# Column sums and row factors in two token halves, a split weight transfer and selection products at the beginning of a hybrid transformer layer

## The chip, the cores and the metric

The kernel runs on one core of a Trainium2 chip. A core has a matrix engine (TensorE, PE in the rows, with its weight loads shown as PEld), VectorE (DVE), ScalarE (ACT), GpSimd (POOL) and SyncE (SP), which here only issues transfers. Each engine works through its own list of instructions in order, and semaphores between the lists carry the dependencies. The metric is the time of one execution on the device in microseconds; the time of a version is the median of several runs.

## What is computed

One layer of a diffusion backbone over 512 latent tokens (x) with 256 context tokens (ctx), 1024 channels. The part that matters here is its start: both streams are normalised by their root mean square and modulated by two vectors per channel that come from a small product with the conditioning vector.

```python
def _rmsnorm(x, gain):
    xf = x.astype(jnp.float32)
    y = xf * lax.rsqrt(jnp.mean(xf * xf, axis=-1, keepdims=True) + EPS)
    return y.astype(x.dtype) * gain

def _modulate(x, gain, shift, scale):
    return _rmsnorm(x, gain) * (1 + scale) + shift

...
    mod = jax.nn.silu(c) @ w_ada[l] + b_ada[l]
    mod_c = jax.nn.silu(c_ctx) @ w_ada[l] + b_ada[l]
    sh1, sc1, g1, sh2, sc2, g2 = jnp.split(mod[:, None, :], 6, axis=-1)
    csh1, csc1, cg1, csh2, csc2, cg2 = jnp.split(mod_c, 6)
    a_lat = _modulate(x, norm_mix[l], sh1, sc1)
    a_ctx = _modulate(xc, norm_mix[l], csh1, csc1)
...
```

Behind that come a combined input projection, a pooling mixer, a bidirectional chunkwise mLSTM, an output projection and a SwiGLU network. The change touches none of these.

## The kernel before

**Layout.** Everything is kept with channels on the 128 partitions and tokens along the free dimension; the 1024 channels are eight blocks of 128, numbered k. Large products are made with three products of split operands (high and low parts), so each weight block and each activation block is split by ScalarE (the high part, a cast) and VectorE (the low part, a subtraction).

**Loads.** SP issues, in the order of the program: the parameter table parm (L104), x in four transfers of two blocks each (L132), the 128x128 identity ident (L137), and then alternately the modulation weights of a block (tile ada, 1 MB, L267) and the first projection weights of a block (tile wr, 384 KB, L330), as far as their three buffers each allow, and the context blocks (tile cx, L381). Before the data arrive, PE multiplies a zero tile by itself (keep_warm, L143); it has shorter groups of such products between its later steps.

**The manual section.** From L255 on, the order of the instructions on PE, ScalarE and VectorE is the one in which the program writes them, until `manual.__exit__`. Outside it a planner orders them. SP and GpSimd are not part of it.

**The sums of squares.** ScalarE squares blocks 0 to 6 of x (L347). VectorE adds squares 1 to 5 to that of block 0 (L349), squares block 7 itself (L350) and adds square 6 to it (L351). PE sums the two results over the channels, with the squares as weights and two columns of ones as the moving operand (L354): for each of four groups of 128 tokens, a column that holds the sum for each token. `power` scales and shifts these (L235, VectorE) and raises them to -1/2 on GpSimd (L237). `rstd_rows` (L245) turns the four columns into a row of 512 factors on all partitions, by a product of the broadcast column with ident.

**The modulation vectors.** For a block k, `mod_rows` (L271) multiplies the activated conditioning vectors of both streams with the block's weights; the eight products of a block lie in four strips of 32 rows of a bank, with four products for r = 0 and four for r = 1 accumulated on them. ScalarE copies the bank out (L274). In `mod_cols`, two transposes on PE (L280) bring it back to channels on partitions, VectorE adds the four strips (L282), and two further operations add the bias and form shift (shm, L284) and scale (sm, L285).

**A stage.** `stage` issues the load of the block's projection weights and splits them (L331, L333); `modulate` forms the normalised and modulated block (L291 on VectorE, L292 on ScalarE for the high part, L295 on VectorE for the low part). `products` (L339) are the first six tiles of the projection, accumulated over the eight blocks in six banks. The loop over k runs the products of block k, with `mod_rows`, `mod_cols` and `stage` of block k + 2 among them.

Of the kernel before, what the change touches and what calls it, by code (L numbers as in the profile page):

```python
# [10 lines left out]
F32 = mybir.dt.float32  # L11
F32R = mybir.dt.float32r
AF = mybir.ActivationFunctionType
ALU = mybir.AluOpType
# [3 lines left out]
P = 128  # L18
D = 1024
KT = D // P  # L20
T = 512
# [19 lines left out]
C_NM, C_NF, C_NFIN = 0, 8, 16  # L41
C_CW, C_CB = 24, 72
C_PS, C_MG, C_C, C_CC, C_BA = 88, 96, 104, 112, 120
NPAR = 168
U0, Q0, K0, O0, G5, G6 = 0, 8, 16, 24, 32, 40
WARM = (32, 2, 2, 2, 0)
# [4 lines left out]
def layer_kernel(ctx: ExitStack, tc, xT, cT, w0, w1, wv0, wv, wada_a, wada_b, par, crow, bg, wpool,  # L51
                 wout, wffi, wffo, icnt, consts, out):
    nc = tc.nc
    V = nc.vector
# [16 lines left out]
    def tl(tag, shape, dtype=F32, bufs=1, align=None):  # L71
        cnt[0] += 1
        return homes[tag].tile(shape, dtype, name=f"{tag}_{cnt[0]}", tag=tag, bufs=bufs, align_bytes=align)

    def S(tag, dtype=F32):
        return tl(tag, [P, T], dtype, BUFS[tag], HALFLINE if tag in shifted else LINE)
# [4 lines left out]
    def PS(tag="ps"):  # L81
        cnt[0] += 1
        return ps.tile([P, 512], F32, name=f"{tag}{cnt[0]}", tag=tag, bufs=4)
# [7 lines left out]
    def small(shape, nm, dtype=F32, home="small"):  # L91
        return homes[home].tile(shape, dtype, name=nm, tag=nm, bufs=1)
# [8 lines left out]


    parm = small([P, NPAR], "parm")
    nc.sync.dma_start(parm, par)  # L104

    def pcol(base, j):
        return parm[:, base + j:base + j + 1]
# [5 lines left out]
    warm = small([P, P], "warm", home="x")  # L113
# [6 lines left out]
    bsc1 = small([P, KT], "bsc1")  # L120
# [8 lines left out]
    x_sb = []  # L129
# [4 lines left out]
    ones = small([P, P], "ones")  # L134
    nc.gpsimd.memset(ones, 1.0)
    ident = small([P, P], "ident")
# [4 lines left out]
    def keep_warm(n, zero):  # L141
        for i in range(n):
            nc.tensor.matmul(wbank[:, :zero.shape[-1]], zero, zero, start=True, stop=True)  # L143
# [52 lines left out]
    class SumSq:  # L196


        q = None
# [51 lines left out]
    ALL = slice(0, T)  # L251
    HALF = (slice(0, T // 2), slice(T // 2, T))
# [4 lines left out]
    stx = SumSq()  # L257
# [2 lines left out]
    mods = small([P, 48], "mods")  # L260
    sm = small([P, KT, 2], "sm")
    shm = small([P, KT, 2], "shm")

    def mod_rows(k):

        raw = tl("ada", [P, KT, 256], F32, 3)
        nc.sync.dma_start(raw.rearrange("p k c -> p (k c)"), wada_a[k])  # L267
        acc = PS()
        for r in range(2):
            for g in range(4):  # L270
                nc.tensor.matmul(acc[32 * g:32 * g + 32, :256], sil[:, 4 * r + g, :], raw[:, 4 * r + g, :],  # L271
                                 start=r == 0, stop=r == 1, tile_position=(0, 32 * g))
        rows = S("tmp")
        nc.scalar.copy(rows[:, :256], acc[:, :256])  # L274
        return rows

    def mod_cols(k, rows):
        bank = PS()
        for w in range(2):
            nc.tensor.transpose(bank[:, w * P:(w + 1) * P], rows[:, w * P:(w + 1) * P], ident)  # L280
        both = tl("rc2", [P, 2, 2], F32, 2)
        V.tensor_reduce(both, bank[:, :2 * P].rearrange("p (w g j) -> p w j g", w=2, g=4)[:, :, 0:2, :],  # L282
                        mybir.AxisListType.X, ALU.add)
        V.tensor_scalar(shm[:, k, :], both[:, 0, :], pcol(C_BA, k), None, ALU.add)  # L284
        V.tensor_scalar(sm[:, k, :], both[:, 1, :], bsc1[:, k:k + 1], pcol(C_NM, k), ALU.add, ALU.mult)  # L285

    def modulate(src, r, scale, shift, h, l, between=None):

# [37 lines left out]
    def stage(k, r):  # L326

        n = len(FIRST) * P
        raw, wh, wl = tl("wr", [P, WMAX], F32, 3), tl("wh", [P, WMAX], F32R, 2, LINE), tl("wl", [P, WMAX], F32R, 2, LINE)
        nc.sync.dma_start(raw[:, :n], w0[k])  # L330
        nc.scalar.copy(wh[:, :n], raw[:, :n])  # L331
        aT.append(modulate(x_sb[k], r, sm[:, k, 0:1], shm[:, k, 0:1], S("a", F32R), S("a", F32R),
                           lambda: V.tensor_sub(wl[:, :n], raw[:, :n], wh[:, :n].bitcast(F32))))  # L333
        w_first.append([(wh[:, i * P:(i + 1) * P], wl[:, i * P:(i + 1) * P]) for i in range(len(FIRST))])
# [9 lines left out]
    bank = PS()  # L344
    sq = [S("tmp") for _ in range(KT)]
    for k in range(KT - 1):
        nc.scalar.activation(sq[k], x_sb[k], AF.Square)  # L347
        if 0 < k < KT - 2:
            V.tensor_add(sq[0], sq[0], sq[k])  # L349
    V.tensor_mul(sq[KT - 1], x_sb[KT - 1], x_sb[KT - 1])  # L350
    V.tensor_add(sq[KT - 1], sq[KT - 2], sq[KT - 1])  # L351
    for t, q in enumerate((sq[0], sq[KT - 1])):
        for i in range(T // P):
            nc.tensor.matmul(bank[:, 2 * i:2 * i + 2], q[:, i * P:(i + 1) * P], ones[:, 0:2], start=t + i == 0,  # L354
                             stop=t == 1, skip_group_check=True)
        if t == 0:
            keep_warm(WARM[1], warm)
    sd = stx.power(bank, T // P)
    rows = mod_rows(0)
    keep_warm(WARM[2], warm)  # L360
    mod_cols(0, rows)
    r = stx.rstd_rows(sd, ALL)
    stage(0, r)
    keep_warm(WARM[3], warm)
    rows = mod_rows(1)
    keep_warm(WARM[4], warm)
    products(0, 0, nf, ((0, 0),))
    mod_cols(1, rows)
    nc.scalar.copy(rs_x, r)
    stage(1, rs_x)  # L370
    for k in range(KT):
        parts = ((0, 0), (0, 1), (1, 0))[0 if k else 1:]
        products(k, 0, nf // 2, parts)
        if k + 2 < KT:
            rows = mod_rows(k + 2)
        products(k, nf // 2, nf, parts)
        if k + 2 < KT:
            mod_cols(k + 2, rows)
            stage(k + 2, rs_x)
        if k < 4:  # L380
            nc.sync.dma_start(cxt[k], cT[:, k * 512:(k + 1) * 512])  # L381
            for e in range(2):
                stc.add(c_sb[2 * k + e], slice(0, TC))
        if k == 4:
            sd = stc.rstd_cols(slice(0, TC))
        if k == 5:
            nc.scalar.copy(rs_c[:, :TC], stc.rstd_rows(sd, slice(0, TC)))
        if k == KT - 2:
            wv_first = vload(wv0, DH + NG, 0)
        if k in (5, 6):  # L390
            ctx_quad(4 * (k - 5))
# [612 lines left out]
    def prepare(j):  # L1004

        a = tl("wr", [P, WMAX], F32, 3)[:, :D]
        b = tl("ur", [P, D], F32, 2)
        nc.sync.dma_start(b, wffi[2 * j + 1])
        nc.sync.dma_start(a, wffi[2 * j])
        a11, a12, a21, a22 = a[:, :T], a[:, T:], b[:, :T], b[:, T:]  # L1010
        p = {}

        def direct(nm, w, dram=None):
            h, l = S("oh", F32R), S("ol", F32R)
            nc.scalar.copy(h, w)
            if dram is None:
                V.tensor_sub(l, w, h.bitcast(F32))
            else:
                nc.scalar.activation(l, w, AF.Copy, scale=-1.0)  # L1019
                nc.gpsimd.dma_start(l, dram, accum_op=ALU.add)  # L1020
            p[nm] = ptiles(h, l)

        def summed(names, o, h, l):
            split(sg[:, o:o + D], h, l)
            for e, nm in enumerate(names):
                p[nm] = ptiles(h, l, e * T)

        yield
        sg = tl("sg", [P, 2 * D], F32, 1, LINE)
        s1, s2, s3, s4 = (sg[:, i * T:(i + 1) * T] for i in range(4))  # L1030
        direct("A11", a11)
        V.tensor_add(s1, a22, a21)
        V.tensor_add(s2, s1, a11)
        summed(("S1", "S2"), 0, wide("gh"), wide("gl"))
        yield
        direct("A12", a12, wffi[2 * j][:, T:])
        yield
        V.tensor_add(s3, a11, a21)
        V.tensor_add(s4, s2, a12)
        yield  # L1040
        summed(("S3", "S4"), D, *(tl(t, [P, WMAX], F32R, 2, LINE)[:, :D] for t in ("wh", "wl")))
        yield
        direct("A22", a22, wffi[2 * j + 1][:, T:])
        yield p
# [70 lines left out]
    sd = st1.rstd_cols(HALF[0])  # L1115
# [3 lines left out]
    r = st1.rstd_rows(sd, HALF[0])  # L1119
# [37 lines left out]
    with tc.manual_schedule(engines={mybir.EngineType.PE, mybir.EngineType.Activation, mybir.EngineType.DVE}):  # L1157
# [3 lines left out]
        sd = st1.rstd_cols(HALF[1])  # L1161
        e.up()
        r = st1.rstd_rows(sd, HALF[1])
# [35 lines left out]
        p = prepare(NP)  # L1199
# [86 lines left out]
    sd = st2.rstd_cols(HALF[0])  # L1286
# [5 lines left out]
    sd = st2.rstd_cols(HALF[1])  # L1292
# [92 lines left out]
```

## Time and profile before

| | |
|---|---|
| median of 3 runs | 887.99 us (887.89 to 888.52) |
| profiled execution, its own time | 889.47 us |
| span of the profiled execution, first to last instruction | 887.7 us |
| mean granted PE clock | 0.999 |
| instructions | 15037 |
| moved by DMA | 120.87 MB, mean 136 GB/s |
| DMA in the first 40 us | 14.70 MB, mean 367 GB/s |

The span is the time between the first and the last instruction of one execution; the execution's own time has something around that. In the rows, `out<-in` names the tiles that an instruction writes and reads, followed by their shapes, a count and durations in microseconds or nanoseconds as stated; `[0.99 <-PE pat L339]` is the idle time of the engine ahead of the instruction and what ended it. The chain is the work that ended last, followed back from the end: each piece is there because the next one waited for it or stood behind it on the same engine. A line number can be that of a helper that several callers use.

### The profile page before, as it was taken

Reading aid. Unit: us, or ns where it says so; the run is one execution under the profiler, and the core shown is the slowest. Engines: PE = TensorE matmul, PEld = TensorE weight load, DVE = VectorE, ACT = ScalarE, POOL = GpSimd, SP = SyncE. Lnnn points to the kernel's source line nnn. Section 1 sums busy time; section 2 is a strip of 40 time slices with the busy share of each in tenths; the row PEclk is TensorE's granted clock in tenths of the full one; section 3 lists DMA queues with packets and bytes.
Section 4 is the critical chain, followed back from the end, with each engine's and each line's share of the span. In section 5 each row is a group of like instructions: output and inputs, shape, how many; then the busy total and the mean of one; then the engine's idle time right before and its main releaser. Section 6 shows DMA issues by size and latency. Waiting matters only on the chain.

```text
span 887.7 us, 15037 instructions
## 1 busy us (share of the span) xinstructions
PE 875.4 (99%) x5920; PEld 796.9 (90%) x5920; DVE 613.8 (69%) x1187; ACT 434.5 (49%) x823; POOL 66.6 (8%) x93
## 2 busy tenths in 40 slices
PE   8999999999999999999999999999999999999996
PEld 7689798899888998889988899999889998899996
DVE  4678676877876787767876767884376753867644
ACT  4464363545345453354545446773146741666542
POOL 0000010010000100001000000110011100111000
PEclk9999999999999999999999999999999999999999
DMA  9853022436252632525443830484266643765402
GB/s 347 324 196 111 25 72 61 166 111 174 75 196 74 196 114 83 163 98 161 137 132 119 286 118 2 128 204 108 83 178 144 155 108 100 196 144 128 135 1 95
DMA packets 41445, 120.87 MB, mean 136 GB/s; under 512 B 4480, under 2 KB 8864, under 8 KB 40352
## 3 DMA queue, kind: packets, MB, share of 16 engines
q1 hardware_dynamic: 35904, 109.96, 38.5%
q0 software_dynamic: 5472, 9.96, 6.7%
q8 instruction: 46, 0.75, 0.3%
q14 instruction: 23, 0.19, 0.1%
HBM read 116.22 MB, written 3.69 MB: 135 GB/s over the span
## 4 chain that ended last, share of the span: by engine, by line
PE 87%; DVE 6%; ACT 3%; DMA 2%; issue 1%; POOL 0%; DVEq 0%; SPq 0%; ACTq 0%; POOLq 0%
PE ps L187 20%; PE ps L188 19%; PE ps L189 19%; PE pat L339 3%; PE ps L571 3%; PE ps L570 3%; PE ps L572 3%; PE pat L187 2%; PE pat L188 2%; PE pat L786 2%; PE pat L189 2%; PE pat L785 2%; PE pat L784 2%; PE ps L339 1%; PE pat L745 1%
## 5 line engine op out<-in xcount | busy, mean ns | idle before, releaser
L157 ACT CAST wh<-wr 128x1024 fp32r<-128x1024 f32 (+3 forms) x78 | 78.8, 1011 | 114.6 <-PE ps L188 87.3
L187 PE MATMUL ps<-a,wh 128*128 128x512 f32 x320 | 125.3, 391 | 0.0
L188 PE MATMUL ps<-a,wh 128*128 128x512 f32 x320 | 124.9, 390 | 0.0
L189 PE MATMUL ps<-a,wl 128*128 128x512 f32 x320 | 124.8, 390 | 0.0
L158 DVE TENSOR_TENSOR wl<-wr,wh 128x1024 fp32r<-128x1024 f32 (+3 forms) x78 | 91.8, 1176 | 43.3 <-ACT wh L157 41.9
L189 PE MATMUL ps<-act,wl 128*128 128x512 f32 (+1 forms) x224 | 77.7, 347 | 0.9 <-DVE wl L158 0.9
L187 PE MATMUL ps<-act,wh 128*128 128x512 f32 (+1 forms) x224 | 77.7, 347 | 0.1
L188 PE MATMUL ps<-act,wh 128*128 128x512 f32 (+1 forms) x224 | 77.5, 346 | 0.0
L189 PEld LDWEIGHTS ps<-a,wl 128*128 128x128 f32 x320 | 60.1, 188 | 12.6
L187 PEld LDWEIGHTS ps<-a,wh 128*128 128x128 f32 x320 | 60.1, 188 | 12.0
L188 PEld LDWEIGHTS ps<-a,wh 128*128 128x128 f32 x320 | 60.1, 188 | 11.6
L1020 POOL DMA_DIRECT2D ol<-in_wffi x38 | 33.4, 887 | 256.1 <-ACT ol L1019 91.6
L187 PE MATMUL ps<-hp,gh 128*128 128x256 f32 x176 | 50.1, 284 | 1.6 <-ACT pat L1058 1.5
L1229 DVE SCALAR_TENSOR_TENSOR x<-ps,lb,x 128x512 f32<-128x512 f32 (+1 forms) x32 | 19.6, 616 | 44.0 <-PE ps L189 43.9
L187 PE MATMUL ps<-hp,oh 128*128 128x256 f32 x176 | 48.9, 278 | 0.1
L189 PE MATMUL ps<-hp,gl 128*128 128x256 f32 x176 | 48.9, 278 | 0.0
L188 PE MATMUL ps<-hp,gh 128*128 128x256 f32 x176 | 48.9, 278 | 0.0
L188 PE MATMUL ps<-hp,oh 128*128 128x256 f32 x176 | 48.7, 277 | 0.0
L189 PE MATMUL ps<-hp,ol 128*128 128x256 f32 x176 | 48.5, 277 | 0.0
L189 PEld LDWEIGHTS ps<-act,wl 128*128 128x128 f32 x224 | 42.2, 188 | 6.8 <-DVE wl L158 1.6
L187 PEld LDWEIGHTS ps<-act,wh 128*128 128x128 f32 x224 | 42.2, 188 | 5.5 <-issue 0.3
L188 PEld LDWEIGHTS ps<-act,wh 128*128 128x128 f32 x224 | 42.2, 188 | 5.3
(341 smaller groups left out, 2629.8 us busy)
## 6 DMA issues: line engine op xcount, KB each, us to landing
wr<-in_w SPq DMA_DIRECT2D x42, 512.0 KB, 3.6
pb<-in_wada_b SPq DMA_DIRECT2D x32, 512.0 KB, 4.2
wr<-in_wffi SPq DMA_DIRECT2D x25, 512.0 KB, 4.2
ur<-in_wffi SPq DMA_DIRECT2D x19, 512.0 KB, 3.9
ol<-in_wffi POOLq DMA_DIRECT2D x38, 256.0 KB, 4.9
ada<-in_wada_a SPq DMA_DIRECT2D x8, 1024.0 KB, 9.5
wr<-in_wffo SPq DMA_DIRECT2D x16, 448.0 KB, 3.5
wr<-in_wout SPq DMA_DIRECT2D x8, 512.0 KB, 3.6
```

The lines of the kernel that those rows point to most:

```text
L157: nc.scalar.copy(wh, raw[:, :n])
L158: V.tensor_sub(wl, raw[:, :n], wh.bitcast(F32))
L187: nc.tensor.matmul(dst, wh, ah, start=first and i == 0, stop=False, skip_group_check=on)
L188: nc.tensor.matmul(dst, wh, al, start=False, stop=False, skip_group_check=on)
L189: nc.tensor.matmul(dst, wl, ah, start=False, stop=last and i == n - 1, skip_group_check=on)
L339: nc.tensor.matmul(acc0[i], w_first[k][i][w], aT[k][x], start=k + w + x == 0, stop=k == KT - 1 and w == 1)
L570: nc.tensor.matmul(acc[:, :n], ah, wh, start=kk == 0, stop=False)
L571: nc.tensor.matmul(acc[:, :n], ah, wl, start=False, stop=False)
L572: nc.tensor.matmul(acc[:, :n], al, wh, start=False, stop=kk == KT - 1)
L784: nc.tensor.matmul(o, sh_, vh[:, s, :], start=n == 0, stop=False)
L1020: nc.gpsimd.dma_start(l, dram, accum_op=ALU.add)
L1229: V.scalar_tensor_tensor(x1[j][:, c], acc[:, c], g2[:, j:j + 1], x1[j][:, c], ALU.mult, ALU.add)
```

## The change

- The table parm is issued from ScalarE's queue instead of SP's.
- A 128x2 matrix pick is made from ident by a reduction on VectorE: column i has a one in each row p with p mod 32 = i, for i = 0 and 1.
- `mod_cols` multiplies the copied rows with pick, two products of two columns, one for the scale and one for the shift. The two transposes and the reduction over strips go; sm and shm are formed from the bank directly, sm first.
- The last square and the last add of the sums of squares are made in two halves of 256 tokens. The column sums of block 0's accumulated squares are made as before. Those of the last square are made for the first half, and `power` is called on it; the sums and the power of the second half come between the first four and the second four modulation products of block 0.
- The modulation weights of block 0 come in two transfers of four channel groups each.
- The row factors are made ahead of `mod_cols(0)`, half by half, each from its own power.

```diff
@@ -101,7 +101,7 @@
 
 
     parm = small([P, NPAR], "parm")
-    nc.sync.dma_start(parm, par)
+    nc.scalar.dma_start(parm, par)
 
     def pcol(base, j):
         return parm[:, base + j:base + j + 1]
@@ -260,13 +260,20 @@
     mods = small([P, 48], "mods")
     sm = small([P, KT, 2], "sm")
     shm = small([P, KT, 2], "shm")
-
-    def mod_rows(k):
+    pick = small([P, 2], "pick")
+    V.tensor_reduce(pick, ident.rearrange("p (g i) -> p i g", g=4)[:, 0:2, :], mybir.AxisListType.X, ALU.add)
+
+    def mod_rows(k, between=None):
 
         raw = tl("ada", [P, KT, 256], F32, 3)
-        nc.sync.dma_start(raw.rearrange("p k c -> p (k c)"), wada_a[k])
+        for h in range(2 if between else 1):
+            n = KT // 2 if between else KT
+            nc.sync.dma_start(raw[:, h * n:(h + 1) * n, :].rearrange("p k c -> p (k c)"),
+                              wada_a[k][:, h * n * 256:(h + 1) * n * 256])
         acc = PS()
         for r in range(2):
+            if r and between:
+                between()
             for g in range(4):
                 nc.tensor.matmul(acc[32 * g:32 * g + 32, :256], sil[:, 4 * r + g, :], raw[:, 4 * r + g, :],
                                  start=r == 0, stop=r == 1, tile_position=(0, 32 * g))
@@ -276,13 +283,10 @@
 
     def mod_cols(k, rows):
         bank = PS()
-        for w in range(2):
-            nc.tensor.transpose(bank[:, w * P:(w + 1) * P], rows[:, w * P:(w + 1) * P], ident)
-        both = tl("rc2", [P, 2, 2], F32, 2)
-        V.tensor_reduce(both, bank[:, :2 * P].rearrange("p (w g j) -> p w j g", w=2, g=4)[:, :, 0:2, :],
-                        mybir.AxisListType.X, ALU.add)
-        V.tensor_scalar(shm[:, k, :], both[:, 0, :], pcol(C_BA, k), None, ALU.add)
-        V.tensor_scalar(sm[:, k, :], both[:, 1, :], bsc1[:, k:k + 1], pcol(C_NM, k), ALU.add, ALU.mult)
+        for w in (1, 0):
+            nc.tensor.matmul(bank[:, 2 * w:2 * w + 2], rows[:, w * P:(w + 1) * P], pick, start=True, stop=True)
+        V.tensor_scalar(sm[:, k, :], bank[:, 2:4], bsc1[:, k:k + 1], pcol(C_NM, k), ALU.add, ALU.mult)
+        V.tensor_scalar(shm[:, k, :], bank[:, 0:2], pcol(C_BA, k), None, ALU.add)
 
     def modulate(src, r, scale, shift, h, l, between=None):
 
@@ -347,19 +351,34 @@
         nc.scalar.activation(sq[k], x_sb[k], AF.Square)
         if 0 < k < KT - 2:
             V.tensor_add(sq[0], sq[0], sq[k])
-    V.tensor_mul(sq[KT - 1], x_sb[KT - 1], x_sb[KT - 1])
-    V.tensor_add(sq[KT - 1], sq[KT - 2], sq[KT - 1])
-    for t, q in enumerate((sq[0], sq[KT - 1])):
-        for i in range(T // P):
-            nc.tensor.matmul(bank[:, 2 * i:2 * i + 2], q[:, i * P:(i + 1) * P], ones[:, 0:2], start=t + i == 0,
-                             stop=t == 1, skip_group_check=True)
-        if t == 0:
-            keep_warm(WARM[1], warm)
-    sd = stx.power(bank, T // P)
-    rows = mod_rows(0)
+    for c in HALF:
+        V.tensor_mul(sq[KT - 1][:, c], x_sb[KT - 1][:, c], x_sb[KT - 1][:, c])
+    for c in HALF:
+        V.tensor_add(sq[KT - 1][:, c], sq[KT - 2][:, c], sq[KT - 1][:, c])
+
+    def column_sums(q, lo, hi, start):
+        for i in range(lo, hi):
+            nc.tensor.matmul(bank[:, 2 * i:2 * i + 2], q[:, i * P:(i + 1) * P], ones[:, 0:2], start=start and i == 0,
+                             stop=not start, skip_group_check=True)
+
+    column_sums(sq[0], 0, 4, True)
+    keep_warm(WARM[1], warm)
+    sds = []
+    column_sums(sq[KT - 1], 0, 2, False)
+    sds.append(stx.power(bank, 2))
+
+    def second_half():
+        column_sums(sq[KT - 1], 2, 4, False)
+        sds.append(stx.power(bank[:, 4:], 2))
+
+    rows = mod_rows(0, second_half)
     keep_warm(WARM[2], warm)
+    r = PS()
+    for h, sd in enumerate(sds):
+        for i in range(2):
+            o = (2 * h + i) * P
+            nc.tensor.matmul(r[:, o:o + P], sd[:, i:i + 1].broadcast_to([P, P]), ident, start=True, stop=True)
     mod_cols(0, rows)
-    r = stx.rstd_rows(sd, ALL)
     stage(0, r)
     keep_warm(WARM[3], warm)
     rows = mod_rows(1)
```

## The prediction

> **What bounds the kernel now.** I read the page first, then the chain of work that ended last in the first 60 us, then the timeline of the same stretch, then the DMA issues with their time to landing.
>
> ```profile
> PE 875.4 (99%) x5920; PEld 796.9 (90%) x5920; DVE 613.8 (69%) x1187; ACT 434.5 (49%) x823; POOL 66.6 (8%) x93
> ```
>
> TensorE (PE) is busy for 99% of the span, so what delays its first real product, or adds work to it, moves the end. The beginning, first the adds of squares in the timeline of VectorE (DVE), then the chain (start, length, what; L354 column sums, L143 warm-keeping, L271 modulation rows, L280 transposes, L245 row factors, L339 products):
>
> ```profile
> 7.42 3.88 DVE L349 TENSOR_TENSOR tmp<-tmp,tmp 128x512 f32<-128x512 f32 x5 [4.08 <-ACT tmp L347]
> ```
>
> ```profile
> 11.44 1.02 PE ps L354 x8
> 12.47 0.55 PE pat L143 x4
> 13.02 0.79 PE ps L354 x8
> 13.81 1.00 PE ps L271 x16
> 14.81 0.64 PE pat L143 x4
> 15.45 0.29 PE ps L280 x2
> 15.74 0.91 PE ps L245 x8
> ...
> 16.67 0.76 DVE tmp L291
> ...
> 18.23 0.73 PE ps L339 x2
> ```
>
> Three pieces are to be seen. Until 11.30 it is the arrival of x and five dependent adds. From 11.44 to 16.65 it is PE work without a gap, 5.21 us. Then 1.56 us of VectorE and ScalarE lead to the first product at 18.23, and from there the chain is PE again.
>
> **The selection matrix, on VectorE.** The new reduction that makes pick reads ident, and it stands in the manual section ahead of the squares and their adds. What matters is when ident is there, and whether VectorE may go past it.
>
> The timelines of SP's queue, of ScalarE (ACT) and of VectorE:
>
> ```profile
> 0.74 0.39 SPq L104 DMA_DIRECT2D parm<-in_par  x1
> 1.19 1.84 SPq L132 DMA_DIRECT2D x<-in_xT  x4
> 3.07 0.65 SPq L137 DMA_DIRECT2D ident<-in_consts  x1
> ...
> 10.26 0.33 SPq L381 DMA_DIRECT2D cx<-in_cT  x1
> ```
>
> ```profile
> 23.93 0.83 ACT L331 CAST wh<-wr 128x768 fp32r<-128x768 f32 x1 [0.99 <-PE pat L339]
> 25.79 0.72 ACT L292 ACTIVATE a<-tmp,shm 128x512 fp32r<-128x512 f32 x1 [1.02 <-DVE tmp L291]
> 26.42 0.40 ACT L212 ACTIVATE tmp<-cx 128x256 f32<-128x256 f32 x1
> ```
>
> ```profile
> 20.14 0.17 DVE L282 TENSOR_REDUCE rc<-ps 128x4 f32<-128x16 f32 x1 [1.18 <-PE ps L280]
> 20.36 0.23 DVE L284 TENSOR_SCALAR shm<-rc,parm 128x2 f32<-128x2 f32 x1
> 20.49 0.28 DVE L285 TENSOR_SCALAR sm<-rc,bsc,parm 128x2 f32<-128x2 f32 x1
> 20.88 0.75 DVE L291 SCALAR_TENSOR_TENSOR tmp<-x,sm,m 128x512 f32<-128x512 f32 x1
> ```
>
> The DMA issues of the start, two answers for two stretches (KB, us to landing):
>
> ```profile
> ident<-in_consts SPq DMA_DIRECT2D x1, 64.0 KB, 7.4
> ```
>
> ```profile
> cx<-in_cT SPq DMA_DIRECT2D x1, 256.0 KB, 11.9
> ```
>
> ident is issued behind all of x and lands at 3.07 + 7.4 = 10.47. Today nobody needs it before 15.45, so this is hidden. In the change its first reader heads VectorE's queue. That the order in this section is that of the program is shown by ScalarE: cx lands at 10.26 + 11.9 = 22.16, yet its square L212 stands behind L331, which waits 0.99 us for a buffer until 23.93, and L212 runs only at 26.42. So I take it that the five adds wait for pick, and pick for ident. Today the first add starts at 7.42.
>
> **parm from ScalarE's queue.** On SP the issue from 0.74 to 1.19 goes, so x, ident and all behind them are issued 0.45 us earlier. The trace has no transfer from ScalarE's queue. At best ident lands 0.45 earlier, at 10.02; if the transfers fill the start anyway, or parm's pieces go between those of x, it stays at 10.47. I take 10.02, since nothing else precedes x. parm itself may land later than now, since it shares the engines with x: VectorE needs it before pick, ScalarE before the squares, of which the adds take the first only at 10.24; that is its cover. ScalarE's own issue (0.39 on SP) lies ahead of its wait for parm and costs nothing.
>
> Then pick starts at about 10.07. The nearest row is L282's reduction of a similar size, 0.17; bounds: nothing, if the next add overlaps it, and 0.3. The adds start at 10.24. They are a dependent series, 7.42 to 11.30 today, 3.88 us, so they end at 14.12: **+2.82** against 11.30. Queued behind pick are only these adds and what follows from them; the squares on ScalarE go on meanwhile.
>
> **Column sums and factors in two halves.** Rows for halves of 256 columns and for the power on GpSimd:
>
> ```profile
> L219 DVE TENSOR_TENSOR tmp<-tmp,tmp x33: 415/425/428, 27.2 to 876.2; 128x256 f32<-128x256 f32 x33
> ```
>
> ```profile
> L237 POOL TENSOR_TENSOR rc<-rc,mhalf x6: 695/705/1147, 14.1 to 879.6; 128x2 f32<-128x2 f32 x5, 128x4 f32<-128x4 f32 x1
> ```
>
> L350 and L351 become four instructions of 0.425. With 0.1 us between dependent ones, the first half is ready at 15.1 and the second at 15.5. PE starts at 14.26 (0.14 after the adds, as today) and by the chain's rows it goes: sums of sq[0] 1.02, warm 0.55, first half of sums 0.40, first four products with ada 0.50, second sums 0.40, second four 0.50, warm 0.64, row factors 0.91, and pick's two products. It reaches the first half of sums at 15.83 and the second at 16.73, both after their data. The powers: sums end at 16.23 and 17.13, VectorE and GpSimd take 0.2 + 0.70, so 17.1 and 18.1; PE wants them at 18.27 and 18.72. All covered, as the power is today; the halves gain nothing, because PE's own list sets this stage. The cover is 0.6 us at the second half; what comes later than that is paid.
>
> **Two transfers of the first modulation weights.** Today L271 starts as soon as the sums before it are done, so its weights are not what ends last; in the change it starts at 16.23, later still. Gain nothing. SP issues one DMA more (0.65 by ident's row), in front of transfers that spend far longer on their way (cx 11.9).
>
> **Selection products.** A product with pick has the form of L229: 128x128 weights, two columns, two instructions each. The chain shows both beside the same six products L339:
>
> ```profile
> 29.66 0.22 PE ps L280 x2
> 29.87 1.39 PE ps L339 x6
> ...
> 46.41 0.22 PE ps L280 x2
> 46.63 0.34 PE ps L229 x4
> 46.97 1.50 PE ps L339 x6
> ```
>
> Four L229 take 0.34 and make the six products behind them 0.11 longer: 0.45. Two transposes take 0.22. So a stage gets **0.23** longer on PE (0.12 if the 0.11 belongs to the pairing, 0.25 at most by the spread of these rows). At stage 0 it is 0.34 in the list above. PE's list is then 5.26 instead of 5.21: **+0.05**, ending at 19.52.
>
> There the order has changed as well. Today reduction, L284 and L285 run while PE makes the row factors, and L291 follows PE's end by 0.02 us. In the change the selection products end last; sm starts 0.04 later, and from L285 to L291 the rows show 0.39 from start to start. L291 starts at 19.95, 0.43 after PE's end: **+0.41**. The first product comes at 19.95 + 1.56 = 21.51 instead of 18.23: **+3.28**.
>
> Seven more stages pay 0.23 on PE, in the stretch where the chain is PE: **+1.6**. The reduction that VectorE saves there stood beside products, at no price. Whether the rest passes the delay on:
>
> ```profile
> PE ps L187 <- ACT pat L1058: 1.5, 2, 1.0
> ```
>
> This is the longest of PE's waits in the whole run (us, times, longest), for a ScalarE step that itself follows from earlier products, so it moves along; were it absorbed, 1.5 would go off the sum.
>
> Sum: 2.82 + 0.05 + 0.41 + 1.6 = **+4.9 us**. The profiled execution took 889.47 (its span, 887.7, and 1.8 around it) and would take 894.4. The median, 887.99, lies 1.48 below it: **892.9**.
>
> **Rivals.** *Pick does not block the adds* (chance 0.13, the side of not slower): the planner places it elsewhere, or ident is there by 6.97, when the first add could start. Then the beginning is −0.45 + 0.05 + 0.41 = 0.0, the seven stages add 1.6, and the time is 889.6; 0.2%, or 1.8 us, is about what can be told from no change, so that is within it. For it: no row shows VectorE itself holding back ready work here; the row is ScalarE's. Against it: that row, and 10.47. The point where it decides is ident's landing, each us of which beyond 6.97 costs a us. If the selection products also cost only 0.12 a stage, it is 888.8.
>
> *The PE pace falls* (0.12): the first warm-keeping ends at 1.36 + 9.21 = 10.57, and the sums start at 14.26 instead of 11.44, so PE is idle for 3.7 us instead of 0.87.
>
> ```profile
> 1.36 9.21 PE L143 MATMUL pat<-warm 128*128 128x128 f32 x64 [1.36 <-DVE warm L114]
> ```
>
> ```profile
> L143 PE MATMUL pat<-warm x76: 275/275/582, 1.4 to 16.8; 128*128 128x128 f32 x76
> ```
>
> ```profile
> 4.00:5.00 1.00, 1.00 (x7) 1.00 (x6) 0.00 (x0) 0.00 (x0) 0.00 (x0) 1.00 0.95 352
> 5.00:6.00 1.00, 1.00 (x10) 1.00 (x10) 0.00 (x0) 0.00 (x0) 0.00 (x0) 1.00 1.02 369
> ```
>
> The second fence gives shortest, median and longest of one, in ns; the third two stretches of 1 us, with PE's instructions in brackets and the granted clock third from the end. Identical products run at about half the pace (582 against 275 ns) from 1.36 until about 5.0, where the count rises; the clock column shows 1.00 for both. If such a phase comes back, the first 3.6 us of the 5.26 do half their work: +1.8, in all 894.7. The rows do not say how long a gap it takes: 0.87 brings no slow phase, the idle time before the kernel did, and 3.7 lies nearer to the former; hence the small chance. The Trainium skill, "TensorE: Matmul & The Clock Gate", section "HAM oscillation — how this bites in real kernels", speaks of gaps over about 3.4 us after which the clock is halved again. By that rule this rival would be likely, as 3.7 is more; the trace agrees on the slow beginning (3.6 us) and has no such gap to show a return.
>
> *The beginning gets faster as meant* (0.03): no wait for ident, and sm's chain hidden: below 886.2.
>
> The forecast keeps 0.72. Its own range: ident and pick 0 to +0.6, list and tail −0.3 to +0.3, stages −0.8 (0.12 each) to +0.15: 891.8 to 894.0. The range of 8 in 10 takes in the slower pace and most of the absorbed wait: 890.3 to 895.0. Faster 0.03, same 0.13, slower 0.84.
>
> **What would show it.** Right: pick's reduction on VectorE ending an idle time of 6 to 7 us, released by ident's DMA, at about 10.1; first add at 10.2 and not near 7.0; PE idle from 10.57 to 14.3; powers of two columns with PE not waiting for them; sm released by the selection products and L291 some 0.4 after them; first product near 21.5; four instructions and some 0.34 in each stage where two took 0.22. Wrong: adds running from 7.0, ident landing before x, products of 0.5 us and more after the gap, or a first product near 18.2 and yet another time.

## The result

The changed kernel takes 898.85 us (median of 4 runs, 897.49 to 900.45) against 888.19 (887.89 to 888.52): a ratio of 1.012, interval 1.0106 to 1.0133, or +10.7 us. It is slower, as forecast, but by more than twice the forecast's +4.9, and lies outside the range. The profiled execution took 900.45 us with a span of 898.6, 10.9 us more than that of before, and the figures below are from it where no other run is named. One run of 2507.8 us of a kernel below and one of 1459.16 us of the kernel before beside the first experiments lie far outside all others and are left out of their times.

The page of the changed kernel: PE's busy time, and the clock that it was granted in 40 slices of 22.5 us.

```profile
PE 886.1 (99%) x5936; PEld 807.0 (90%) x5936; DVE 612.6 (68%) x1183; ACT 436.0 (49%) x823; POOL 66.4 (7%) x94
...
PEclk8899999999999999999999999999999999999999
```

PE is as full as before, with 10.7 us more of busy time and 16 instructions more. Its added time is thus not idle time; it was busy and slower. The 8 in the first two slices says where to look. The chain of work that ended last, from the issue of ident on (start, length, what; L361 column sums, L278 modulation rows, L380 row factors, L287 selection products, L343 products, L143 warm-keeping):

```profile
2.85 6.23 DMA ident<-in_consts
...
9.10 0.17 DVE pick L264
9.26 0.61 DVE tmp L353
...
13.06 0.14 issue
13.19 1.13 PE ps L361 x8
14.32 1.06 PE pat L143 x4
15.38 0.64 PE ps L361 x4
16.03 1.01 PE ps L278 x8
17.04 0.94 PE ps L361 x4
17.98 1.01 PE ps L278 x8
18.99 1.15 PE pat L143 x4
20.14 1.71 PE ps L380 x8
21.85 0.65 PE ps L287 x4
22.50 1.06 PE pat L143 x4
...
25.42 1.15 PE ps L343 x2
26.58 1.46 PE pat L343 x4
28.04 0.34 PE ps L287 x4
...
32.46 0.34 PE ps L287 x4
```

Two things are to be seen. ident's landing now heads the chain, through pick and the adds, and the sums start at 13.19 where they started at 11.44: +1.75. Then, from the warm-keeping behind them on, the pieces of PE take up to twice the time that their like took before: the four warm-keeping products 1.06 for 0.55, the row factors 1.71 for 0.91, the first four selection products 0.65 where the later ones take 0.34. PE's list, 5.21 before, is 9.31 here (13.19 to 22.50). The first product comes at 25.42 for 18.23.

The windows show why. The columns are the length, the busy time of PE, PEld, DVE, ACT and POOL with instructions in brackets, then the granted clock, the DMA share and GB/s.

```profile
13.50:14.00 0.50, 0.50 (x7) 0.50 (x6) 0.50 (x3) 0.00 (x0) 0.00 (x0) 0.97 1.04 442
14.00:14.50 0.50, 0.50 (x3) 0.50 (x4) 0.39 (x2) 0.00 (x0) 0.00 (x0) 0.50 0.93 393
...
27.00:27.50 0.50, 0.50 (x3) 0.41 (x2) 0.00 (x0) 0.14 (x1) 0.00 (x0) 0.50 1.14 371
27.50:28.00 0.50, 0.50 (x4) 0.37 (x4) 0.00 (x0) 0.00 (x0) 0.00 (x0) 0.87 0.86 238
```

The clock falls from 1.00 to 0.50 within the first window and comes back within the last. 0.97 means 0.03 us at half, so it fell at 13.97; 0.87 means 0.13 us at half, so it rose at 27.63: 13.66 us. The fall follows a stretch in which PE had nothing to do, between the end of the first warm-keeping and the sums:

```profile
1.36 10.15 PE L143 MATMUL pat<-warm 128*128 128x128 f32 x64 [1.36 <-DVE warm L114]
13.19 1.13 PE L361 MATMUL ps<-ones,tmp 128*128 128x2 f32 x8 [1.68 <-DVE tmp L353]
```

These are rows of PE's timeline; 1.68 is the idle time ahead of the sums, 0.87 before. It is shorter than the 3.7 us of the prediction on both sides: the adds end earlier, because ident landed earlier, and the warm-keeping ends later (10.15 us for 9.21).

By the step on the chain at which each stage's transposes (before) or selection products (after) stand, the difference grows as follows: 19.89 to 28.04 is +8.15, 24.08 to 32.46 +8.38, 29.66 to 38.28 +8.62, and so on by 0.22 a stage to +9.50 at the last (52.45 to 61.95). So of the 10.9 us some 9.7 are there when the projection's first pass ends: 1.75 for the wait, 8.15 less 1.75 and less 0.4 of list and tail, or 6.0, for the clock, and seven stages of 0.22. The other 1.2 us come later, in code that the change does not touch.

The 6.0 is a remainder; the stretch allows it, since 13.66 us at half clock can cost 6.83 at most. It is the price in this one execution, which is the slowest of the four and has the lowest mean clock, 0.990. The other three, at 0.994 and 0.995, took 897.49 to 899.32, so that the price in them was smaller; they have no profile.

### The profile page after: what moved, and what is told of

It reads as the page before. It is cut to its first block, busy times and chain, and to the rows that moved or that the text cites. A ratio compares the mean times of both kernels' runs of the same rounds, so it can differ in the third digit from the quotient of the medians.

```text
span 898.6 us, 15069 instructions
## 1 busy us (share of the span) xinstructions
PE 886.1 (99%) x5936; PEld 807.0 (90%) x5936; DVE 612.6 (68%) x1183; ACT 436.0 (49%) x823; POOL 66.4 (7%) x94
## 4 chain that ended last, share of the span: by engine, by line
PE 91%; DVE 4%; ACT 2%; DMA 1%; issue 1%; SPq 0%; DVEq 0%; ACTq 0%
PE ps L187 20%; PE ps L189 20%; PE ps L188 20%; PE pat L343 3%; PE ps L589 3%; PE ps L591 3%; PE ps L590 3%; PE pat L805 2%; PE pat L803 2%; PE pat L804 2%; PE pat L187 2%; PE pat L188 2%; PE pat L189 2%; PE ps L343 1%; PE pat L763 1%; PE pat L764 1%
## 5 line engine op out<-in xcount | busy, mean ns | idle before, releaser
L187 PE MATMUL ps<-a,wh 128*128 128x512 f32 x320 | 125.2, 391 | 0.0
L187 PE MATMUL ps<-act,wh 128*128 128x512 f32 (+1 forms) x224 | 78.0, 348 | 0.3 <-DVE tmp L1102 0.3
L187 PEld LDWEIGHTS ps<-a,wh 128*128 128x128 f32 x320 | 60.1, 188 | 11.9
L188 PEld LDWEIGHTS ps<-a,wh 128*128 128x128 f32 x320 | 60.1, 188 | 11.6
L187 PE MATMUL ps<-hp,gh 128*128 128x256 f32 x176 | 50.0, 284 | 1.0 <-ACT pat L1077 1.0
L187 PE MATMUL ps<-hp,oh 128*128 128x256 f32 x176 | 48.9, 278 | 0.1
L187 PEld LDWEIGHTS ps<-act,wh 128*128 128x128 f32 x224 | 42.2, 188 | 5.7 <-issue 0.5
```

Of the source, the lines that this page charges most:

```text
L187: nc.tensor.matmul(dst, wh, ah, start=first and i == 0, stop=False, skip_group_check=on)
L188: nc.tensor.matmul(dst, wh, al, start=False, stop=False, skip_group_check=on)
```

## The experiments

In each, the kernel before was timed beside it on the same chip, and ratios are to it. The questions: is it the gap (theory A) or the new thin products, many of them two columns wide, of the halves and of pick (theory B) that brings the half clock, and where do the late microseconds come from?

### pick's reduction behind the adds

The changed kernel with that one instruction moved; the wait goes, all else of the change stays.

```diff
     pick = small([P, 2], "pick")
-    V.tensor_reduce(pick, ident.rearrange("p (g i) -> p i g", g=4)[:, 0:2, :], mybir.AxisListType.X, ALU.add)
...
         V.tensor_add(sq[KT - 1][:, c], sq[KT - 2][:, c], sq[KT - 1][:, c])
+    V.tensor_reduce(pick, ident.rearrange("p (g i) -> p i g", g=4)[:, 0:2, :], mybir.AxisListType.X, ALU.add)
```

> The changed kernel, with the reduction that makes pick moved behind the adds of squares on VectorE; all else as changed. Theory A (the wait for ident delays the adds, PE then stands idle and its clock is halved for what follows): the adds start with the squares again, PE idles under 1 us, no stretch at a granted clock of 0.50, and what is left is the longer selection products: 889 to 890.5. Theory B (the clock falls because the new order of PE's beginning is made of thin products, whatever the gap): still a stretch at 0.50 and at least 895.

893.65 us (892.96 to 893.93), ratio 1.0058 [1.0040, 1.0076]. Its chain, in which L286 are the selection products and L342 the products:

```profile
1.36 10.31 PE pat L143 x64
11.68 0.79 PE ps L362 x8
...
18.82 0.73 PE ps L342 x2
...
24.89 0.34 PE ps L286 x4
...
30.70 0.34 PE ps L286 x4
```

PE goes from warm-keeping into the sums without a gap, the clock is 0.998 as a mean in every run, and half of the loss is gone. The first product is 0.59 late instead of 7.19. So the same thin products, without the gap, bring no half clock, which speaks for A. But the time is 3 us above A's range. From 24.89 to 30.70 a stage takes 5.81 where before took 5.59 (24.08 to 29.66 by the chain), which is the 0.22 again, and at the last stage the two differ by 1.9 (54.38 against 52.45). The rest of the 5 us had to be elsewhere.

### Longer warm-keeping, in two sizes

The changed kernel with the wait, but more products ahead of the sums.

```diff
-WARM = (32, 2, 2, 2, 0)
+WARM = (40, 2, 2, 2, 0)
```

> The changed kernel with 40 instead of 32 products in the first warm-keeping, some 1.7 us more of it, so that PE is busy until the column sums; pick still holds the adds back. Theory A: the clock stays at 1.00, only the delay of the adds (1.75), sm's tail (0.4) and the selection products (1.6) are left: 891.5 to 892.5. Theory B: clock falls as before, 897 to 900.

901.75 us (899.32 to 906.69), 1.0158 [1.0118, 1.0197], slower than the change itself, as neither theory said. PE's timeline shows that the edit missed its aim:

```profile
1.36 10.58 PE L143 MATMUL pat<-warm 128*128 128x128 f32 x80 [1.36 <-DVE warm L114]
13.86 1.23 PE L361 MATMUL ps<-ones,tmp 128*128 128x2 f32 x8 [1.92 <-DVE tmp L353]
```

80 instructions took hardly longer than 64 in the changed kernel (10.58 to 10.15), because the slow phase with which the program begins ended sooner here, at about 4.3 us for about 7, by the number of these products in each half microsecond. A gap of 1.92 us was left, and the clock was half behind it from 14.54 to 28.19 (13.65 us). It decides nothing between A and B. So the next kernel took 48.

```diff
-WARM = (32, 2, 2, 2, 0)
+WARM = (48, 2, 2, 2, 0)
```

> The changed kernel with 48 instead of 32 products in the first warm-keeping, enough for PE to be busy until the column sums wherever the slow first phase ends (40 were not). Theory A: the clock is 1.00 throughout; left are the delay of the adds by pick (1.75, or up to 1 more where the products run over), sm's tail, the selection products and the addresses: 893 to 895.5. Theory B (thin products lower the clock in any case): 897 to 900 at a clock of 0.99.

896.55 us (895.64 to 897.07), 1.0087 [1.0074, 1.0101]. Chain and windows of this run:

```profile
1.36 12.74 PE pat L143 x96
14.10 0.79 PE ps L361 x8
...
21.25 0.73 PE ps L343 x2
```

```profile
14.00:15.00 1.00, 1.00 (x11) 1.00 (x11) 0.77 (x3) 0.00 (x0) 0.00 (x0) 1.00 0.98 408
15.00:16.00 1.00, 1.00 (x16) 0.85 (x15) 0.16 (x1) 0.00 (x0) 0.00 (x0) 1.00 1.10 451
```

The wait is there, the gap is not, and the thin products run at full clock: the first product is 3.02 late, which is warm-keeping past the adds (sums at 14.10 for 11.44, 2.66) and the tail. The loss against before is 7.8 us, 1 above A's range; 3.0 and seven stages (1.5) explain 4.5, and the remaining 3.3 have to be found outside the beginning. Against the changed kernel, 2.9 us are gained although the sums start 0.9 later (14.10 for 13.19), so by the medians the half clock costs some 3.8 us there, an estimate from the two kernels.

### The wait alone, in the kernel before

Only the reduction and its tile, at their place; nobody reads pick, and nothing else changes.

```diff
     sm = small([P, KT, 2], "sm")
     shm = small([P, KT, 2], "shm")
+    pick = small([P, 2], "pick")
+    V.tensor_reduce(pick, ident.rearrange("p (g i) -> p i g", g=4)[:, 0:2, :], mybir.AxisListType.X, ALU.add)
```

> The kernel before, with nothing added but the reduction that makes pick at its place (its result is not used). Theory A: VectorE waits for ident, the adds come 2 to 3 us late, PE idles 2 us or more and the clock is halved for some 13 us: 895 to 899. Theory B: only the delay, 890 to 891.5, at a clock of 1.00.

894.87 us (893.65 to 896.13), 1.0073 [1.0058, 1.0089]: +6.4 us from one instruction of 0.17. Its chain, the row of the sums in PE's timeline, then its windows:

```profile
3.07 7.33 DMA ident<-in_consts
...
10.42 0.17 DVE pick L264
...
14.52 1.02 PE ps L356 x8
...
24.27 0.66 PE ps L341 x2
```

```profile
14.52 1.02 PE L356 MATMUL ps<-ones,tmp 128*128 128x2 f32 x8 [3.55 <-DVE tmp L351]
```

```profile
16.00:17.00 1.00, 1.00 (x8) 1.00 (x8) 0.00 (x0) 0.00 (x0) 0.00 (x0) 0.61 1.04 435
17.00:18.00 1.00, 1.00 (x10) 0.67 (x14) 0.16 (x1) 0.00 (x0) 0.36 (x1) 0.50 0.94 396
...
23.00:24.00 1.00, 1.00 (x18) 0.48 (x17) 1.00 (x2) 0.67 (x1) 0.00 (x0) 0.97 0.45 188
```

ident lands at 10.40, the sums are 3.1 late, PE is idle for 3.55 us ahead of them, and with none of the change's thin products the clock is half from 16.22 to 23.06 (6.84 us). That is A, whose 895 was missed by 0.1; B's number was missed by 3.4. But the stretch is half of the 13 us that A expected, and so is its price: the first product is 6.0 late (24.27 for 18.23), 3.1 for the wait and 3.0 for the clock.

The mean clock of this execution is 0.994. In the three unprofiled runs of the changed kernel it is 0.994 and 0.995, so a price of about 3 us in those is an estimate from this trace, near the 3.8 by the medians.

The added tile may itself have moved tiles behind it. From the first product to the end of the span this execution takes 870.1 us and that of the kernel before 869.5, so little of the 6.4 can lie there.

### A gap without a wait

The kernel before with fewer warm products, so that PE is idle and nothing else is late.

```diff
-WARM = (32, 2, 2, 2, 0)
+WARM = (28, 2, 2, 2, 0)
```

> The kernel before with 28 instead of 32 products in the first warm-keeping: PE idles some 1.7 us ahead of the column sums instead of 0.87, as long as in the changed kernel, and nothing else is changed. Theory A in its simple form (a gap of this length is enough): a stretch at a clock of 0.50 and 893 to 896. Theory B, or a gap that has to fall in a certain place: 887.9 to 888.5 in all or some of the runs, with a clock of 1.00.

891.36 us (888.17 to 892.87 in ten runs), 1.0027 [1.0013, 1.0041]: below A's numbers, above B's. The fastest run, 888.17, is the profiled one, and its PE timeline shows no gap:

```profile
1.36 9.36 PE L143 MATMUL pat<-warm 128*128 128x128 f32 x56 [1.36 <-DVE warm L114]
10.68 1.02 PE L354 MATMUL ps<-ones,tmp 128*128 128x2 f32 x8
```

By the pace of these products the first slow phase happened to last until about 7.2 us there, and the sums could start 0.76 earlier than in the trace of before, so that 56 instructions filled the time. The other nine took 889.39 to 892.87 at mean clocks of 0.993 to 0.998, against 0.999. No profile of those exists, so that they had a gap is argued from the clock, not shown.

### ident ahead of x

The other cure: the changed kernel with ident issued first (and a 32-byte tile whose reason comes below).

```diff
+    ident = small([P, P], "ident")
+    nc.sync.dma_start(ident, consts[:, :P])
...
-    ident = small([P, P], "ident")
-    nc.sync.dma_start(ident, consts[:, :P])
...
+    spacer = small([P, 8], "spacer")
+    nc.gpsimd.memset(spacer, 0.0)
```

> The changed kernel at the old addresses, with ident issued ahead of x; pick keeps its place ahead of the adds. Theory A (it is ident's landing that counts, not pick's place): ident lands by 4 us, the adds start with the squares, the clock stays at 1.00, and the time is that of pick made late at these addresses: 889.5 to 891. If pick's place in VectorE's list costs by itself: 895 and more.

891.82 us (890.39 to 895.60), 1.0043 [1.0027, 1.0058]. VectorE's timeline, then the row of the sums in PE's:

```profile
3.92 0.16 DVE L266 TENSOR_REDUCE pick<-ident 128x2 f32<-128x8 f32 x1
...
7.54 3.87 DVE L355 TENSOR_TENSOR tmp<-tmp,tmp 128x512 f32<-128x512 f32 x5 [3.31 <-ACT tmp L353]
```

```profile
11.56 1.02 PE L363 MATMUL ps<-ones,tmp 128*128 128x2 f32 x8 [1.05 <-DVE tmp L355]
```

pick waits for nobody, the adds start at 7.54 by their squares, and five of six runs keep a clock of 0.998 or 0.999, among them the profiled one, whose gap of 1.05 us did no harm; the sixth (895.60) shows 0.993. So pick's place in VectorE's list costs little once ident is there. The median is 0.8 us above A's range, and the reason is not shown. That x lands later behind ident cannot be told from one trace: the adds start at 6.49 to 7.52 in the traces with x first and no wait for pick.

### Addresses of the tiles

The late loss suggested the memory, since the change removes two buffers of rc2 (64 bytes) and adds pick (32 bytes), and so moves the tiles that are placed behind them. The windows of the products that read the tile act, near the end of the run, on one chip: first the kernel with fewer warm products (addresses of before), then the one with pick late (addresses of the change). The columns are length, busy time with instructions, clock, DMA share and GB/s.

```profile
850.00:865.00 15.00, 15.00 (x134) 1.00 0.00 1
```

```profile
850.00:865.00 15.00, 15.00 (x128) 1.00 0.00 1
```

The same products, at full clock in both, get through 134 against 128 in 15 us (5%). That was the ground for theory C, by which the moved addresses cost this time; by theory D they cost nothing. But the later traces do not bear this sign out. The same window of the kernel with parm alone (below), in which no tile is changed:

```profile
850.00:865.00 15.00, 15.00 (x130) 1.00 0.00 1
```

The kernel before has 135, and on the chip of this run the kernels with ident first and with the transposes kept, both at the old addresses, have 135 and 134. So these products have a faster and a slower pace at the same addresses, and the first two fences do not show what the addresses cost. What tests C are the times of three kernels. In the first an unused tile puts the old addresses back, in the kernel with pick late:

```diff
     pick = small([P, 2], "pick")
+    spacer = small([P, 8], "spacer")
+    nc.gpsimd.memset(spacer, 0.0)
```

> As the run with pick made late, plus an unused tile of 32 bytes a partition, with which every tile behind it stands at the address that it has in the kernel before (the change frees 64 bytes and takes 32, so all of them move by -32, and some that are aligned by -64 or -256). Theory C (some 2 us of the rest are paid far behind the beginning, by products that read operands from moved addresses): the products at the end (842 to 876 us) run at their old pace again, and the time falls from 893.6 to 891.3 to 892.2. Theory D (addresses do not matter, the rest is in the beginning): 893 to 894.

890.37 us (889.54 to 891.85), 1.0018 [1.0008, 1.0028]: +1.6 where +5.2 had been without the tile, below the range of either theory. The products at the end did not run at the faster pace again, as C had said they would: 129 in the same window.

The second moves the tiles of the kernel before by 32 bytes and changes no instruction's work:

```diff
-        both = tl("rc2", [P, 2, 2], F32, 2)
+        both = tl("rc2", [P, 2, 2], F32, 1)
```

> The kernel before with one buffer instead of two for the small tile rc2, which alone moves all tiles behind it by -32 bytes, to the addresses that they have in the changed kernel; no instruction is added or left out. Theory C: 889.5 to 891, with the loss behind 690 us. Theory D: 888.0 to 888.8.

891.06 us (889.90 to 892.12), 1.0027 [1.0017, 1.0037]: +2.4 us, D's number missed, and C's upper end by 0.1. The tile's writer and both its readers are on VectorE, which takes them in the program's order, so one buffer adds no wait on another engine. In its trace the time from the first product to the end of the span is 871.9 us. It is 869.5 in the kernel before, 868.9 with 28 warm products and 870.0 with parm alone, which have the old addresses; so the loss lies behind the beginning. That it comes from the addresses is concluded from what the edit leaves unchanged. The third gives the change as it is its old addresses:

```diff
     pick = small([P, 2], "pick")
+    spacer = small([P, 8], "spacer")
+    nc.gpsimd.memset(spacer, 0.0)
     V.tensor_reduce(pick, ident.rearrange("p (g i) -> p i g", g=4)[:, 0:2, :], mybir.AxisListType.X, ALU.add)
```

> The changed kernel with all tiles at the addresses of the kernel before (the unused tile of 32 bytes), pick still holding back the adds. Theory A and C together: the wait, the slow clock and the selection products stay, the price of the addresses goes: 896 to 897.5 against 898.85. Were the addresses nothing: 898 to 900.

897.90, 896.54 and 895.36 us, ratio 1.0091 [1.0076, 1.0105] or +8.1, against +10.7 without the tile; the median, 896.54, is inside the range of A and C together. The three differences, 3.6, 2.4 and 2.6 us, agree within their errors, and 2.4 also fits what was missing with 48 warm products: 4.5 and 2.4 are 6.9, inside that interval of 6.6 to 9.0 us. Where they fall is not known. Of the 2.4 of the second kernel act's products account for some 0.5: they take 41.6 us from the first to the last start of L187's there, and 41.0 on the same chip in the first kernel and in the next one below.

### The other parts one by one

Selection products alone, in the kernel before, with pick behind the adds and the old addresses:

```diff
+    pick = small([P, 2], "pick")
+    spacer = small([P, 8], "spacer")
...
-            nc.tensor.transpose(bank[:, w * P:(w + 1) * P], rows[:, w * P:(w + 1) * P], ident)
...
+            nc.tensor.matmul(bank[:, 2 * w:2 * w + 2], rows[:, w * P:(w + 1) * P], pick, start=True, stop=True)
...
+    V.tensor_reduce(pick, ident.rearrange("p (g i) -> p i g", g=4)[:, 0:2, :], mybir.AxisListType.X, ALU.add)
```

> The kernel before with the selection products alone, pick being made behind the adds, and the addresses kept by an unused tile; column sums, row factors, loads and the order of PE's beginning as before. By the prediction's term: 0.23 on PE in each of eight stages, so 889.6 to 890.1 at a clock of 1.00. If the transposes cost as much as the products: 888.2.

890.88 us (889.88 to 891.49), 1.0024 [1.0014, 1.0034]: +2.1, where eight stages of 0.23 make 1.8. The time is 0.8 above the expected range; the kernel before took 888.72 beside it, 0.5 more than the 888.19 above.

The complement: everything of the change but pick, so the halves, the two transfers, the new order and parm on ScalarE's queue, with transposes and old addresses.

```diff
...
-        for w in (1, 0):
-            nc.tensor.matmul(bank[:, 2 * w:2 * w + 2], rows[:, w * P:(w + 1) * P], pick, start=True, stop=True)
...
+            nc.tensor.transpose(bank[:, w * P:(w + 1) * P], rows[:, w * P:(w + 1) * P], ident)
```

> The changed kernel with the transposes and the reduction over strips kept, so with no pick at all: parm on ScalarE's queue, sums and factors in halves, two transfers of the first weights and factors ahead of the modulation columns are left, at the old addresses. By the prediction's terms 0.45 is gained with parm and 0.4 lost at the tail: 887.9 to 889. If the halves pay as such: below 887.5.

889.19 us (888.29 to 889.90), 1.0008 [0.9999, 1.0016]. No gain, and 0.2 above the expected range. Its first product is at 18.48, 0.25 late, though its sums start 0.56 earlier (10.88) than in the trace of before: from the sums to the first product the new order takes 7.60 for 6.79.

parm on ScalarE's queue alone, in the kernel before:

```diff
-    nc.sync.dma_start(parm, par)
+    nc.scalar.dma_start(parm, par)
```

> The kernel before with parm issued from ScalarE's queue and nothing else changed. By the prediction's term x comes 0.45 earlier and the time falls to 888.0 to 888.5 against 888.7 of the runs beside it, within what can be told from no change. If parm, landing 2 us later beside x, holds back ScalarE's squares: 889 to 890.

888.13 us (887.25 to 889.58), 0.9996 [0.9988, 1.0005]. In its trace the adds start 0.7 earlier (6.72) and the first product 0.47 earlier (17.76). That is no sign of parm's queue: with parm on SP's queue the adds start at 6.49 and 6.58 in the kernels with one buffer and with 28 warm products. The time moves by less than can be told.

The parts add up: wait and clock 6.4 (alone in the kernel before), addresses 2.4, selection products 2.1, the other parts 0.7, in all 11.6 against 10.7, each part with an error of about 1. Some of the agreement is luck, since the wait was 3.1 in the first of these kernels and 1.75 in the profiled execution of the change.

## Why the prediction was right or wrong

**pick blocks the adds.** Right in its mechanism. The reduction on VectorE ends an idle time, released by ident's DMA:

```profile
9.10 0.17 DVE L264 TENSOR_REDUCE pick<-ident 128x2 f32<-128x8 f32 x1 [3.58 <-DMA ident<-in_consts]
...
22.54 0.28 DVE L288 TENSOR_SCALAR sm<-ps,bsc,parm 128x2 f32<-128x2 f32 x1 [4.36 <-PE ps L287]
22.73 0.21 DVE L289 TENSOR_SCALAR shm<-ps,parm 128x2 f32<-128x2 f32 x1
22.86 0.74 DVE L295 SCALAR_TENSOR_TENSOR tmp<-x,sm,ps 128x512 f32<-128x512 f32 x1
```

The term was too large: 1.75 instead of 2.82, since ident landed at 9.08, not 10.02. The prediction moved the issue by 0.45 and took over the landing of before, 7.4 us after the issue. The issue moved by 0.22 (3.07 to 2.85), and ident took 6.2. One execution does not give this time well: in five traces with the same loads as before it is 6.4, 6.7, 7.1, 7.3 and 7.4. So the size of this term was in part a matter of chance.

**The PE pace falls.** This is the step that failed: the sum left out a slower clock behind PE's gap. It stood as a rival with a chance of 0.12 and a price of 1.8 us. All four runs show a mean clock of 0.990 to 0.995; the price is 6.0 in the profiled one and, by the estimates above, 3 to 4 at the median. Two arguments were wrong. The first, that a gap of 3.7 us lies nearer to 0.87, which does no harm: 1.68 us sufficed, in the changed kernel, and 1.92 with 40 products. The Trainium skill, "TensorE: Matmul & The Clock Gate", section "HAM oscillation — how this bites in real kernels", with its gaps over about 3.4 us, pointed to the right rival. The trace of the wait alone agrees, with 3.55 us; in the changed kernel 1.68, half that length, was enough, and the measurement decides. The second, that a slow phase would last 3.6 us as at the start. It lasted 13.66 us with the change, and 6.84, half as long, with the wait alone. What the runs show beside the number: in the changed kernel the clock came back only after the first large products (25.42 on), and in the kernel with the wait alone after a stretch of the same short products as before. That the thin and halved products made the half clock last twice as long is consistent with this and was not tested by itself.

**PE's list.** 5.26 was right at full clock: in the kernel with pick late it is 5.24 (11.68 to the end of L286 at 16.92).

**The tail.** Right: from the end of the selection products (22.50) to L295 (22.86) it is 0.36, against 0.41, and 0.02 before, by the rows above.

**Selection products.** Right: 0.22 a stage by the chains, 0.23 predicted; alone, in eight stages and in the old order, they cost 2.1 us where 1.8 follow from 0.23.

**Halves, two transfers, parm.** Right that they gain nothing: 1.0008 and 0.9996. The powers are not on the chain. That parm might land later was right too, by the DMA issues of the changed kernel (KB, us to landing):

```profile
parm<-in_par ACTq DMA_DIRECT2D x1, 84.0 KB, 4.1
ident<-in_consts SPq DMA_DIRECT2D x1, 64.0 KB, 6.2
```

It took 4.1 us for 2.0 before, and its cover held.

**What had no term.** Moved tiles, 2.4 us. Nothing in the prediction asked what the removal of rc2's buffers and a new small tile do to the tiles behind them, and no view of before would have given the price.

With 1.75 for the wait, 0.4 for list and tail, 1.5 for the stages, 6.0 for the clock and about 1.2 after that, the profiled execution's +10.9 is accounted for. The 1.2 is the difference of two single executions; why it is less than the 2.4 of the addresses by the medians is not shown. Without the clock and the addresses the sum would have been 3.7, near the 4.9 of the forecast less its error in ident's landing.

Still open: why a shift of some bytes costs time, and where it falls; why act's products have two paces at the same addresses; how short a gap is harmless (0.87 was in the trace of before and 1.05 in that of ident ahead of x, 1.68 was not), and what makes the half clock last 6.84 us or twice that; and why the first slow phase ends at another time in each execution.

None of these versions beats the kernel before by more than can be told.

## What to carry to other kernels

An instruction of 0.17 us at the head of an in-order queue costs what its input costs: look up when that input lands before placing it, and place it behind whatever does not need it. Where PE's clock depends on keeping it busy, price a wait not by its length but by the half clock that may follow, here 6 us in the profiled execution, and by estimate 3 to 4 at the median, for a gap of 1.7. When a change adds or removes even a small tile, keep the addresses of the rest (a spacer does) before comparing instructions.

## What the runs showed of the hardware

- The granted clock fell after an idle time of 1.68 us between the warm products and the sums, 0.78 us after PE had begun to work again, and stayed at 0.50 for 13.66 us, in which PE was busy. After 3.55 us in another kernel it stayed at 0.50 for 6.84. Idle times of 0.87 and 1.05 were not followed by a fall.
- With 96 warm instructions and no gap, the same wait and the same thin products ran at 1.00.
- The slow phase at the start of the program ended between about 4.3 and 7.2 us after the span's start in different executions, by the pace of the same products, so 80 warm instructions once took 10.58 us and 64 took 10.15: a warm-up that is counted in products leaves gaps of differing length.
- With one buffer of a small tile less, which moves the tiles behind it by 32 bytes or more, unchanged instructions took 2.4 us more (interval of the ratio 1.0017 to 1.0037), behind the first products.
- One group of products got through 135 in 15 us in one execution and 130 in another, at full clock in both and with no tile of the program changed between them.
- A table of 84 KB issued on ScalarE's queue at the same time (0.74) as on SP's landed after 4.1 us instead of 2.0, while 2 MB of x went through SP's.
